# A hybrid decoder layer: four reciprocal square roots moved to GpSimd's power, and the sums of head norm and LayerNorm given out one at a time

## The chip, the cores and the metric

One core of one Trainium2 chip runs the whole program as one launch. The metric is the time of one execution on the device, in microseconds (us). The core's engines are called PE (TensorE, with its weight loads as PEld), DVE (VectorE), ACT (ScalarE), POOL (GpSimd) and SP (SyncE, which here issues the DMAs).

## The reference

One layer of a decoder is computed in fp32 for a prompt of 1024 tokens and for 8 sample sequences of 8 tokens (1088 tokens in all), with 1024 features:

```python
h = rmsnorm(x, norm_mix_pre)                      # x * rsqrt(mean(x*x) + EPS) * g
(a_b, a_c, a_u, b_p, c_q, c_f, c_i, c_g, d_a, d_g) = jnp.split(h @ w_in, 10, axis=-1)   # G = 256 each
ya = a_b * causal_dwconv(a_c * a_u, ...)          # A: short gated conv
yb = pooled @ w_grp * pool_scale                  # B: multi-scale pooling
# C: a scan with a matrix state, then per head (4 heads of 64):
o  = o * lax.rsqrt(jnp.mean(o * o, axis=-1, keepdims=True) + EPS) * norm_g
yc = o * jax.nn.silu(zg)
# D: GLU, 31-tap conv, then LayerNorm and swish
yd = jax.nn.silu(layernorm(conv + conf_b, conf_ln_g, conf_ln_b))
x  = x + rmsnorm(jnp.concatenate([ya, yb, yc, yd], axis=-1) @ w_out, norm_mix_post)
h  = rmsnorm(x, norm_ffn_pre)
x  = x + rmsnorm((jax.nn.silu(h @ w_gate) * (h @ w_up)) @ w_down, norm_ffn_post)
```

The outputs are x and the final states of the mixers.

## The kernel before

Features lie on the partitions in tiles of 128 and tokens lie along the free axis. Large products take three passes: an operand is split into a high part (`xh`, `wop`'s first half) and a low part (`xl`, `wop`'s second half), and the products high by high, high by low and low by high are summed in PSUM. The program runs through these stages:

- **Norm of x.** The 1088 tokens are cut into three chunks of 256, 384 and 448. `x_sq` squares a chunk on ACT (L217), `x_norm` makes the reciprocal square root of each token's mean square and scales the rows (L68), and `x_split` transposes them on PE (L234) and splits them into `xh` (ACT, L235) and `xl` (DVE, L71).
- **Phase 1, input projection and mixers.** Twenty units of 128 columns of `w_in` are multiplied (L984; a set of three products on 256, 384 and 448 tokens for each contraction tile and pass). The mixers' work on the other engines is written as Python generators. After every few products `hook` lets them run for about as long as the products take; a generator that must wait for another engine yields `None` and goes on at a later turn. PE and DVE keep the order in which this code issues their instructions (`tc.manual_schedule`); the orders of ACT and SP in this phase are set by a scheduler.
- **Mixer sums.** `stats_rstd` sums squares over features for each token: nine small products (L394) into a PSUM tile `sm`, of which there are two, and then `rsqrt_steps`. It serves the head norm (`hd`, once for each half j of the heads) and the LayerNorm (`ln`). `L916` is the last state update of mixer C; its result, also in an `sm` tile, is added to the state `s` on DVE.
- **Outputs of the mixers.** The last unit takes its contraction tiles in the order 6, 7, 2, 3, 0, 1, 4, 5, and `put_y` replaces `xh` and `xl` of a tile by the split outputs of the mixers (ACT cast L1030, DVE subtraction `xl<-y,xh` L65) once the unit is through with it. The last unit's own result is a gate (`z`, ACT L434) that is multiplied into an output tile by three DVE instructions `y<-y,z`.
- **Phase 2, output projection** (L1116): for the first token piece, one output tile after another takes the contraction tiles in the same order. The weights' halves are split by ACT (L1007) and DVE (`wop<-raw,wop`).
- **FFN.** Gate, up and down projections by Strassen's scheme and plain products (the groups at L1388 and L1593). The last token chunks of 448, 384 and 256 end in `finish`: token sums of squares on PE (L1082), a reciprocal square root (`rs_f0`, `rs_f1`, `rs_f2`), its transposition to all partitions on PE (`spread`, L178), scaling by the gain and the residual on DVE and POOL, and a store. In this last stage ACT, DVE, PE and POOL all keep the written order.

`rsqrt_steps` makes the reciprocal square root on DVE: one instruction for the argument m, two for an integer seed, and three Newton steps of three instructions, 12 in all, each working on the result of one just before it.

Of the kernel before, what the change touches and what calls it, by code (L numbers as in the profile page):

```python
# [13 lines left out]
ALU = mybir.AluOpType  # L14
# [3 lines left out]
P = 128  # L18
SEQ = 1024
NB, TB = 8, 8            # sample sequences, tokens of each  # L20
NT = SEQ + NB * TB       # 1088 tokens in all, the prompt's first
D = 1024
KT = D // P              # 8 feature tiles of the model
G = 256
NF = 22                  # hidden tiles of the FFN
EPS = 1e-6
F_MIN = 1e-20
CH = [(0, 256), (256, 384), (640, 448)]     # token chunks, one PSUM bank each
NG = SEQ // P            # 8 prompt groups of 128 tokens; the sample's 64 are group 8
GRP = [(i * P, P) for i in range(NG)] + [(SEQ, NB * TB)]  # L30
GO = [i * P for i in range(NG)] + [NT - P]     # groups of 128 tokens, the last overlapping
PW = 272
NPAIR = 8                                  # pairs of hidden tiles that go through the down projection by Strassen
HG = [range(16, 19), range(19, 22)]        # groups of the other hidden tiles
DC = [(0, 448), (448, 384), (832, 256)]     # token chunks of the down projection
PIECES = (0, 544, 272, 816)                # token pieces, as pairs of the two halves
# [3 lines left out]
# columns of the packed per-feature parameters  # L40
# [7 lines left out]
# columns of the constants that depend on shapes alone  # L48
# [4 lines left out]
def body(ctx, tc, xn, xT, win, wout, wgu, wdn, par, con, msk, poolw, s_conv, s_pool, s_hgrn, s_conf,  # L53
# [40 lines left out]
    V.memset(ones, 1.0)  # L94

# [4 lines left out]
    def rsqrt_steps(src, shape, scale, tag):  # L100
        """1 / sqrt(src * scale + EPS) on a compact tile: integer seed and three Newton steps."""
# [20 lines left out]

    def load_w(src, kt=4):
        raw = T(wp, [P, 4 * P], "raw").rearrange("p (k c) -> p k c", c=P)
        SY.dma_start(raw, src)
        return raw

    def split_w(raw, hl):
        """Weights into their high and low parts."""
        S.copy(hl[:, 0], raw)  # L130
        TT(hl[:, 1], raw, f32(hl[:, 0]), ALU.subtract)

    def mm_part(ps, hls, k, c):
        """One contraction tile's three passes on one token chunk."""
# [5 lines left out]
    # =====================================================================================  # L140
    # phase 1: input projection and the four mixers
    # =====================================================================================
# [20 lines left out]
    # lower bound of the forget gate: softmax over the one layer, its running sum less its first row  # L163
# [12 lines left out]
    def bcast(ps, col, n, off=0):  # L176
        """A per-token column to all partitions, feature-major."""
        PE.transpose(ps[:, off:off + n], col[:n].to_broadcast([n, P]), ident[:n, :n])  # L178
# [18 lines left out]
    # RMSNorm of x by tokens, then to feature-major and split; x lies where the mixers' outputs come later  # L197
# [22 lines left out]
    def x_norm(c, ss):  # L220
        idx = x_idx(c)
        for r in rsqrt_steps(ss[:, :len(idx)], [P, len(idx)], 1.0 / D, f"x{CH[c][1]}"):
            yield
# [76 lines left out]
    # A generator yields what its last step costs the vector engine, None where it has to wait for another engine.  # L300
    # The work of crit comes first, that of bulk fills what is left; due is what the last products call for.
    MM = 0.1135                               # a product's share of the schedule, one piece wide
# [3 lines left out]
    def fill(work, blocked):  # L306
        """A step of the first work that has any; what it costs."""
# [12 lines left out]
    def hook(budget):  # L320
        """As much of the other engines' work as fits under a stretch of products."""
# [23 lines left out]
    def until(ready):  # L345
        """Work without products until a condition holds."""
# [8 lines left out]
    def take(**want):  # L355
        """Waits for free buffers of the rings and counts them as taken."""
# [8 lines left out]
    def pe(cost):  # L365
        """The tensor engine's time for small products, in which the vector engine may do more."""
        state["budget"] += cost
# [21 lines left out]
    def stats_rstd(sq, scale, tag, rhs=None, w=1):  # L389
        """Sums over features of feature-major tiles, per token, then their rsqrt: [tokens, group * w]."""  # L390
        yield from take(sm=1)
        st = sm()
        for i, go in enumerate(GO):
# [3 lines left out]
            if i % SP == SP - 1:  # L397
                yield None
# [10 lines left out]
    # masks and state tiles  # L409
# [7 lines left out]
    qz = [T(mp, [P, 2, 256], f"qz{i}") for i in range(2)]      # each head's queries among zeros of the other's  # L417
# [6 lines left out]
    def pchunks(ps):  # L424
        """The prompt's part of a unit's products, chunk by chunk."""
# [180 lines left out]
    def b_pool(j, p, s):  # L606
        yield from wait(2 * LW)
        yield from take(h=2)
        # doubling sums; the last step only where the partition's window asks for it
# [80 lines left out]
    def hgrn(j):  # L690
# [12 lines left out]
        # blocks of four tokens, the decay taken relative to each block's second token  # L703
        for hf, (o, n) in enumerate(((0, 512), (512, NT - 512))):
# [21 lines left out]
            # their masked products; the heads' halves of the array work side by side  # L726
# [27 lines left out]
        # prefix products to q, suffix products to k, in blocks that double  # L754
# [1084 lines left out]
```

## Time and profile before

| quantity | value |
|---|---|
| median of 3 runs (lowest to highest) | 1198.31 us (1196.83 to 1198.78) |
| span of the profiled execution | 1193.7 us |
| median less that span | 4.6 us |
| PE busy | 1153.1 us, 97% |
| DVE busy | 885.4 us, 74% |
| ACT busy | 451.0 us, 38% |
| POOL busy | 139.9 us, 12%, 130 instructions |
| chain that ended last, by engine | PE 81%, DVE 10%, issue 3%, DMA 2%, ACT 2%, POOL 1% |

The span reaches from the profiled execution's first instruction to its last. No total beyond the span is given for that one execution, so steps are taken against the span, and the 4.6 us up to the median is taken as a constant. In the page's slices PEclk is the clock that was granted to PE, in tenths of full speed: it reads 9 in nearly all of the 40 slices and 8 in the 11th and in the last. A line such as `342.52 1.89 DVE L65 ... x3` gives the start and the length of a stretch of three instructions of one kind, both in us, and a bracket behind it gives the idle time before and what ended it. Where a matmul is busy, its start and end overlap its neighbours'.

### The profile page before, as it was taken

What the parts mean: (1) busy time and instruction counts of PE and PEld (TensorE: products, weight loads), DVE (VectorE), ACT (ScalarE), POOL (GpSimd) and SP (SyncE); (2) the same over time, 40 slices, a digit from 0 to 9 for tenths busy, and PEclk for the clock granted to TensorE, in tenths of its full rate; (3) what the DMA queues carried; (4) which work ended last, traced back from release to release, by engine and by line L of the source; (5) the groups of instructions that cost most, each with busy time, mean ns of one, the idle gap of its engine ahead of it and who ended that gap; (6) DMA issues with size and microseconds to landing.
All of it is one profiled execution on the core that took longest, in us unless ns stands there. A gap on an engine that the chain in (4) does not pass through costs nothing.

```text
span 1193.7 us, 21654 instructions
## 1 busy us (share of the span) xinstructions
PE 1153.1 (97%) x8476; PEld 1116.1 (94%) x8476; DVE 885.4 (74%) x1770; ACT 451.0 (38%) x964; POOL 139.9 (12%) x130
## 2 busy tenths in 40 slices
PE   5999999999999999999999999999999999999995
PEld 4899899998999999999999999999999989999994
DVE  6468979997674678786677576666675679998687
ACT  7534322243264453443333233233334653333321
POOL 1000000000000000000000000000002363447234
PEclk9999999999899999999999999999999999999998
DMA  7011112211135123021323233133234453434732
GB/s 261 34 38 24 36 37 68 41 36 40 30 130 199 39 74 127 24 95 67 115 101 105 70 111 118 60 114 110 91 122 135 141 178 121 137 109 125 259 108 88
DMA packets 93333, 116.89 MB, mean 98 GB/s; under 512 B 23664, under 2 KB 62192, under 8 KB 93232
## 3 DMA queue, kind: packets, MB, share of 16 engines
q1 hardware_dynamic: 93232, 115.52, 30.1%
q8 instruction: 66, 1.08, 0.4%
q14 instruction: 35, 0.29, 0.1%
HBM read 86.61 MB, written 28.88 MB: 97 GB/s over the span
## 4 chain that ended last, share of the span: by engine, by line
PE 81%; DVE 10%; issue 3%; DMA 2%; ACT 2%; POOL 1%; SPq 0%; DVEq 0%; ACTq 0%; POOLq 0%
PE p L1388 30%; PE mm L984 18%; PE p L1116 8%; PE p L1593 7%; PE p L1297 5%; PE p L1481 4%; DVE wop L65 3%; DVE raw L65 2%; PE mm L137 2%; PE sm L798 2%; DVE t L65 1%; DMA raw<-wgu 1%; ACT wop L1007 1%; DVE xl L65 1%; DMA raw<-hx 1%
## 5 line engine op out<-in xcount | busy, mean ns | idle before, releaser
L65 DVE TENSOR_TENSOR wop<-raw,wop 128x512 fp32r<-128x512 f32 (+2 forms) x296 | 210.2, 722 | 137.9 <-ACT wop L1007 127.5
L1007 ACT CAST wop<-raw 128x512 fp32r<-128x512 f32 (+1 forms) x240 | 143.4, 604 | 267.0 <-PE p L1388 151.7
L1388 PE MATMUL p<-xh,wop 128*128 128x272 f32 x1216 | 235.1, 288 | 0.0
L1388 PEld LDWEIGHTS p<-xh,wop 128*128 128x128 f32 x1216 | 193.5, 188 | 0.0
L1388 PE MATMUL p<-t,wop 128*128 128x272 f32 x912 | 179.6, 290 | 1.7 <-DVE u L65 1.6
L984 PE MATMUL mm<-xh,wop 128*128 128x256 f32 (+2 forms) x864 | 178.5, 335 | 0.0
L1388 PE MATMUL p<-xl,wop 128*128 128x272 f32 x608 | 175.6, 289 | 0.0
L1388 PEld LDWEIGHTS p<-t,wop 128*128 128x128 f32 x912 | 145.6, 188 | 2.4 <-DVE u L65 2.4
L984 PEld LDWEIGHTS mm<-xh,wop 128*128 128x128 f32 x864 | 139.5, 190 | 6.6 <-issue 1.1
L1388 PE MATMUL p<-x,wop 128*128 128x272 f32 x456 | 131.4, 288 | 0.0
L1388 PEld LDWEIGHTS p<-xl,wop 128*128 128x128 f32 x608 | 114.4, 188 | 0.0
L1116 PE MATMUL p<-xh,wop 128*128 128x272 f32 x512 | 99.2, 290 | 2.0 <-DVE wop L65 2.0
L984 PE MATMUL mm<-xl,wop 128*128 128x256 f32 (+2 forms) x432 | 99.0, 338 | 0.0
L65 POOL TENSOR_TENSOR x<-raw,x 128x544 fp32r<-128x544 f32 (+3 forms) x18 | 24.9, 1389 | 626.4 <-ACT x L1521 613.1
L65 DVE TENSOR_TENSOR raw<-raw,raw 128x512 f32<-128x512 f32 (+1 forms) x123 | 83.7, 690 | 4.5 <-DMA raw<-wgu 3.3
L1388 PEld LDWEIGHTS p<-x,wop 128*128 128x128 f32 x456 | 85.9, 188 | 0.0
L1593 PE MATMUL p<-xh,wop 128*128 128x272 f32 x456 | 82.1, 288 | 2.3 <-DVE acc L65 1.2
L71 DVE SCALAR_TENSOR_TENSOR y<-u,prm,y 128x1024 f32<-128x1024 f32 (+1 forms) x68 | 82.6, 1224 | 2.2 <-ACT y L570 0.7
L1116 PEld LDWEIGHTS p<-xh,wop 128*128 128x128 f32 x512 | 81.0, 188 | 2.2 <-DVE wop L65 2.2
L1593 PE MATMUL p<-xl,wop 128*128 128x272 f32 x456 | 81.5, 288 | 1.2 <-DVE x L65 0.9
L1297 PE MATMUL p<-xh,wop 128*128 128x272 f32 x384 | 74.1, 289 | 0.0
L1116 PE MATMUL p<-xl,wop 128*128 128x272 f32 x256 | 73.9, 289 | 0.0
(322 smaller groups left out, 2021.0 us busy)
## 6 DMA issues: line engine op xcount, KB each, us to landing
raw<-wgu SPq DMA_DIRECT2D x88, 256.0 KB, 2.7
raw<-hx SPq DMA_DIRECT2D x56, 272.0 KB, 2.7
raw<-win SPq DMA_DIRECT2D x40, 256.0 KB, 3.0
hx<-x SPq DMA_DIRECT2D x64, 136.0 KB, 1.8
raw<-wdn SPq DMA_DIRECT2D x32, 256.0 KB, 2.9
raw<-wdn SPq DMA_DIRECT2D x32, 192.0 KB, 2.9
x<-xT SPq DMA_DIRECT2D x8, 544.0 KB, 6.2
x<-x SPq DMA_DIRECT2D x8, 544.0 KB, 3.0
```

Source lines behind the costliest of these rows:

```text
L65: (eng or V).tensor_tensor(out, a, b, op)
L71: (eng or V).scalar_tensor_tensor(out=out, in0=a, scalar=s, in1=b, op0=op0, op1=op1)
L137: PE.matmul(ps[c][:, :n], hl[:, wi, kk], X[k][:, o:o + n], start=k == 0 and wi == 0 and X is XH, stop=k == KT - 1 and wi == 1)
L798: PE.matmul(ps[:rows, g * P:(g + 1) * P], kk[:, o:o + rows], qz[hf][:, :, g * 64:(g + 1) * 64], start=True, stop=True, skip_group_check=True)
L984: PE.matmul(ps[c][:, :w], hl[:, wi, kk], X[k][:, o:o + w], start=k == order[0] and wi == 0 and X is XH, stop=k == order[-1] and wi == 1)
L1007: S.copy(hl[:, 0], raw)
L1116: PE.matmul(ps[nt][:, :PW], WO[nt][k // 4][:, wi, kk:kk + P], X[k][:, o:o + PW], start=k == korder[0] and wi == 0 and X is XH, stop=k == k ...
L1297: PE.matmul(ps[r][:, :PW], w[:, wi, (k % 4) * P:(k % 4 + 1) * P], X[k][:, o:o + PW], start=k == 0 and wi == 0 and X is XH, stop=k == KT - ...
L1388: PE.matmul(ps[:, :PW], wop[:, wi, kk * P:(kk + 1) * P], x(kk, xi), start=first and kk == 0 and wi == 0 and xi == 0, stop=kk == 3 and wi == 1,
L1481: PE.matmul(ps[:, :n], wd[:, wi, kk * P:(kk + 1) * P], hops[k][xi][:, o:o + n], start=first and kk == 0 and wi == 0 and xi == 0, stop=not ...
L1593: PE.matmul(ps[:, :PW], ws[name][wi][q], x[:, xi, pr], start=first and q == 0 and wi == 0 and xi == 0, stop=q == 1 and wi == 1, skip_group ...
```

## The change

The diff is cut to the lines that act (it also takes comments out, which shifts line numbers by about 12):

```diff
     ones = T(const, [P, P], "ones")
     V.memset(ones, 1.0)
+    mhalf = T(const, [P, 1], "mhalf")
+    V.memset(mhalf, -0.5)
...
+    def rsqrt_pow(src, shape, scale, tag):
+        m, y = T(const, shape, f"rs_{tag}m"), T(const, shape, f"rs_{tag}y")
+        TS(m, src, scale, EPS)
+        GP.tensor_tensor(y, m, mhalf[:, :1].to_broadcast(shape), ALU.pow)
+        return y
...
     def x_norm(c, ss):
         idx = x_idx(c)
-        for r in rsqrt_steps(ss[:, :len(idx)], [P, len(idx)], 1.0 / D, f"x{CH[c][1]}"):
-            yield
+        args = ss[:, :len(idx)], [P, len(idx)], 1.0 / D, f"x{CH[c][1]}"
+        if c == 0:
+            r = rsqrt_pow(*args)
+        else:
+            for r in rsqrt_steps(*args):
+                yield
...
     def stats_rstd(sq, scale, tag, rhs=None, w=1):
...
             pe(0.22)
-            if i % SP == SP - 1:
-                yield None
+            yield None
...
     def finish(c, sqa, x1t):
         o, n = DC[c]
         st, gr = stats(sqa, n)
-        for r in rsqrt_steps(st, [P, len(gr)], 1.0 / D, f"f{c}"):
-            yield
+        r = rsqrt_pow(st, [P, len(gr)], 1.0 / D, f"f{c}")
+        yield
         rb = spread(r, gr)
...
-            for _ in range((11, 1, 1, 2, 2, 1, 2, 0)[j]):
+            for _ in range((1, 1, 1, 2, 2, 1, 2, 0)[j]):
```

For the first chunk of x and for the three last norms, DVE makes m, and POOL raises it to the power -0.5 in one instruction on a tile of 128 partitions by 2 to 4 columns. In the loop over output tiles, the first tile's 11 turns for the last norm become one, so that the other steps of `finish` stand at the same output tiles as before. In `stats_rstd`, the generator now gives up its turn after every one of its nine sums, and not after every third.

The first place is the end of the program, the norm of the last 256 tokens (`rs_f2`), on DVE. Before:

```order
L68 TENSOR_SCALAR rs_f2m_13387<-p_13384 128x2 [waits PE_49]
L68 TENSOR_SCALAR rs_f2y_13389<-rs_f2m_13387 128x2 [waits DVE_49]
L68 TENSOR_SCALAR rs_f2h_13388<-rs_f2m_13387 128x2
L65 TENSOR_TENSOR rs_f2a_13390<-rs_f2y_13389 128x2 [waits DVE_49]
L65 TENSOR_TENSOR rs_f2a_13390<-rs_f2a_13390,rs_f2h_13388 128x2 [waits DVE_49]
L71 SCALAR_TENSOR_TENSOR rs_f2y_13389<-rs_f2a_13390,rs_f2y_13389 128x2 [waits DVE_49]
```

Two more such Newton steps follow there. After, on POOL at the same place (`acc` and `t` are residual additions, of the chunk before ahead of the power and of this chunk behind it):

```order
L65 TENSOR_TENSOR acc_1308_10252<-acc_1308_10252,xl_1681_12851 128x384 [waits DMAHW1_49,DVE_49,Pool_49]
L65 TENSOR_TENSOR acc_1309_10253<-acc_1309_10253,xl_1681_12851 128x384 [waits DVE_49,Pool_49]
L129 TENSOR_TENSOR rs_f2y_13354<-rs_f2m_13353,mhalf_76 128x2 [waits DVE_49]
L65 TENSOR_TENSOR t_0_1302_10246<-t_0_1302_10246,xh_1710_13106 128x256 [waits DMAHW4_49,DVE_49]
L65 TENSOR_TENSOR t_0_1304_10248<-t_0_1304_10248,xl_1711_13108 128x256 [waits DMAHW5_49,DVE_49]
```

Eleven DVE instructions are gone, and one on POOL stands between DVE's `rs_f2m` and PE's `spread`.

The second place is on PE, at the last state update of mixer C in the second half of the heads (`L916`, after: `L928`). The names `sm` with a number are PSUM tiles, `cst` marks a head-norm sum and `ones` a LayerNorm sum. Before:

```order
L984 MATMUL mm_2697<-xh_9_81,wop_2619 128x448
L916 MATMUL sm_2831<-z_2809,khat_2755 64x512 [waits DVE_49,PE_49,Activation_49]
L916 MATMUL sm_2831<-z_2809,khat_2755 64x512 [waits DVE_49]
L394 MATMUL sm_2840<-cst_72,h_1566 128x2 [waits PE_49,Activation_49]
L394 MATMUL sm_2840<-cst_72,h_1566 128x2 x2
L984 MATMUL mm_2695<-xh_10_82,wop_2619 128x256
```

After:

```order
L996 MATMUL mm_2857<-xh_6_79,wop_2711 128x448
L928 MATMUL sm_2877<-z_2842,khat_2798 64x512 [waits DVE_49,Activation_49]
L928 MATMUL sm_2877<-z_2842,khat_2798 64x512 [waits DVE_49]
L407 MATMUL sm_2886<-cst_72,h_1556 128x2 [waits DVE_49,PE_49]
L407 MATMUL sm_2835<-ones_74,h_2618 128x1
L996 MATMUL mm_2855<-xl_14_87,wop_2711 128x256
```

LayerNorm's tile `sm_2835` is in use when the head norm's sums begin, the state update holds the other tile, and the first head-norm sum now waits for DVE.

The third place is on DVE, between the mixers and the output projection. Before (tiles 82, 83, 78, 79, 76, 77, 80 and 81 of `xh` are contraction tiles 6, 7, 2, 3, 0, 1, 4 and 5):

```order
L65 TENSOR_TENSOR xl_18_90<-y_26_104,xh_10_82 128x1088 [waits Activation_49]
L65 TENSOR_TENSOR xl_19_91<-y_27_105,xh_11_83 128x1088 [waits Activation_49]
L65 TENSOR_TENSOR xl_14_86<-y_22_100,xh_6_78 128x1088 [waits Activation_49]
L65 TENSOR_TENSOR xl_15_87<-y_23_101,xh_7_79 128x1088 [waits Activation_49]
L65 TENSOR_TENSOR xl_12_84<-y_20_98,xh_4_76 128x1088 [waits Activation_49]
L65 TENSOR_TENSOR xl_13_85<-y_21_99,xh_5_77 128x1088 [waits Activation_49]
L65 TENSOR_TENSOR wop_3151<-raw_3153,wop_3151 128x512 [waits DMAHW7_49]
L65 TENSOR_TENSOR y_25_103<-y_25_103,z_3147 128x256 [waits DVE_49,Activation_49]
```

There, the other two `y<-y,z`, three `wop` and then `xl` of tiles 4 and 5 follow. After (every tile's number is one higher):

```order
L65 TENSOR_TENSOR xl_15_88<-y_23_102,xh_7_80 128x1088
L65 TENSOR_TENSOR wop_3135<-raw_3137,wop_3135 128x512 [waits DMAHW5_49]
L65 TENSOR_TENSOR y_26_105<-y_26_105,z_3131 128x256 [waits DVE_49,Activation_49]
L65 TENSOR_TENSOR y_26_105<-y_26_105,z_3131 128x384 [waits DVE_49,Activation_49]
L65 TENSOR_TENSOR y_26_105<-y_26_105,z_3131 128x448 [waits DVE_49,Activation_49]
L65 TENSOR_TENSOR wop_3136<-raw_3138,wop_3136 128x512 [waits DMAHW6_49]
L65 TENSOR_TENSOR wop_3148<-raw_3150,wop_3148 128x512 [waits DMAHW3_49,PE_49]
L65 TENSOR_TENSOR wop_3149<-raw_3151,wop_3149 128x512 [waits DMAHW4_49,PE_49,Activation_49]
L65 TENSOR_TENSOR xl_16_89<-y_24_103,xh_8_81 128x1088
L65 TENSOR_TENSOR xl_13_86<-y_21_100,xh_5_78 128x1088
L65 TENSOR_TENSOR xl_14_87<-y_22_101,xh_6_79 128x1088
L65 TENSOR_TENSOR xl_17_90<-y_25_104,xh_9_82 128x1088 [waits Activation_49]
```

The `xl` of contraction tiles 3, 0 and 1 now stand behind `y<-y,z` and the `wop`, together with tile 4's; only tiles 6, 7 and 2 stand ahead.

## Prediction

> **What bounds the kernel now.** The page comes first: busy time by engine, then the chain of work that ended last.
>
> ```profile
> PE 1153.1 (97%) x8476; PEld 1116.1 (94%) x8476; DVE 885.4 (74%) x1770; ACT 451.0 (38%) x964; POOL 139.9 (12%) x130
> ...
> PE 81%; DVE 10%; issue 3%; DMA 2%; ACT 2%; POOL 1%; SPq 0%; DVEq 0%; ACTq 0%; POOLq 0%
> ```
>
> PE bounds nearly all of the span. Taking DVE work away is therefore worth something only where PE waits for it, and a change of order costs where it makes PE wait. PE can also lose time while it counts as busy: at a lower granted clock. So the second view is the busy time by 4 us stretches around the mixers' sums (columns: stretch, its length, busy PE, PEld, DVE, ACT, POOL, granted clock, DMA share, GB/s).
>
> ```profile
> 304.00:308.00 4.00, 4.00 (x33) 3.94 (x32) 2.35 (x5) 0.00 (x0) 0.00 (x0) 1.00 0.41 69
> 308.00:312.00 4.00, 4.00 (x19) 3.91 (x19) 1.77 (x7) 0.62 (x1) 0.00 (x0) 0.52 0.00 1
> 312.00:316.00 4.00, 4.00 (x16) 3.80 (x17) 3.52 (x22) 0.06 (x1) 0.00 (x0) 0.63 0.00 0
> 316.00:320.00 4.00, 4.00 (x22) 3.29 (x21) 0.76 (x2) 2.67 (x4) 0.00 (x0) 1.00 0.38 131
> ```
>
> The clock falls to half soon after 308 and is back before 316. The loss is 4.00 x (1 - 0.52) + 4.00 x (1 - 0.63) = 1.92 + 1.48 = 3.4 us. What ran just ahead is in the timeline of PE, third view.
>
> ```profile
> 302.08 1.08 PE L916 MATMUL sm<-z,khat 64*64 64x512 f32 x4
> 303.08 0.83 PE L394 MATMUL sm<-cst,h 128*128 128x2 f32 x6
> ...
> 304.85 0.66 PE L984 MATMUL mm<-xh,wop 128*128 128x256 f32 x3
> 305.35 0.72 PE L394 MATMUL sm<-cst,h 128*128 128x2 f32 x6
> 305.93 0.81 PE L394 MATMUL sm<-ones,h 128*128 128x1 f32 x6
> 306.60 0.74 PE L984 MATMUL mm<-xh,wop 128*128 128x256 f32 x3
> 307.18 0.72 PE L394 MATMUL sm<-cst,h 128*128 128x2 f32 x6
> 307.77 1.06 PE L394 MATMUL sm<-ones,h 128*128 128x1 f32 x6
> ```
>
> PE is never idle here, but from 304.85 to about 308.2 there are only two sets of wide products (starts 304.85 and 306.60, about 0.5 us each until the next group starts), some 1.1 us in 3.4, or a third. The rest are sums 1 or 2 columns wide. The clock falls right behind it. I read this as a grant that follows how many columns pass through PE, and not the busy share, which was full.
>
> **The change, part by part.**
>
> *Sums one at a time, the clock.* Nine turns in place of three spread the 18 instructions of each norm's sums between sets of wide products: one sum (about 0.12 us of PE, from the 0.7 us of three) behind each set or two. No stretch of 3.4 us then holds two thirds of sums, and the drop at 308 should go: -3.4 us. Bounds: 0, if it moves to a neighbouring stretch, and -3.4.
>
> *Sums one at a time, PE's wait for a PSUM tile.* There are two `sm` tiles. With LayerNorm's sums started earlier and ending later, its tile is held when mixer C's last state update takes the other. Head norm's first sum stands right behind that update on PE, and must now wait until DVE has read it.
>
> ```profile
> 303.23 1.40 DVE L65 TENSOR_TENSOR s<-s,sm 64x512 f32<-64x512 f32 x2 [0.17 <-PE sm L916]
> ```
>
> Before, PE started the sums at 303.08 while DVE read until 303.23 + 1.40 = 304.63. After, PE stands still for those two additions; everything behind the sum in PE's order waits too. From 303.08 to 304.63 it is 1.55; the addition's start can come a little sooner against PE. I take +1.4, bounds 0.7 (one addition, the other under PE's tail) and 1.6.
>
> *The transition to the output projection.* As a later end of the generators, the order on DVE changes: `xl` of contraction tiles 3, 0 and 1 stand behind `y<-y,z` and the `wop` splits. The rows of before, DVE first, then the group of the wide `xl`, then PE:
>
> ```profile
> 341.12 1.48 DVE L65 TENSOR_TENSOR y<-y,z 128x256 f32<-128x256 f32 x3
> 342.52 1.89 DVE L65 TENSOR_TENSOR wop<-raw,wop 128x512 fp32r<-128x512 f32 x3
> 344.32 2.69 DVE L65 TENSOR_TENSOR xl<-y,xh 128x1088 fp32r<-128x1088 f32 x5
> ```
>
> ```profile
> L65 DVE TENSOR_TENSOR xl<-y,xh 128x1088 fp32r<-128x1088 f32 x7 | 9.0, 1291 | 2.0 <-ACT xh L1030 1.9
> ```
>
> ```profile
> 340.89 0.28 PE L1116 MATMUL p<-xh,wop 128*128 128x272 f32 x1
> 341.01 0.29 PE L1116 MATMUL p<-xl,wop 128*128 128x272 f32 x1
> 343.26 0.52 PE L1116 MATMUL p<-xh,wop 128*128 128x272 f32 x2 [1.96 <-DVE wop L65]
> ...
> 345.66 0.39 PE L1116 MATMUL p<-xl,wop 128*128 128x272 f32 x1
> ```
>
> Before, PE waits 1.96 us for the `wop` split and then runs on; the product at 345.66 is the first to need `xl` of tile 4, which DVE makes from 344.32 to about 345.6. After, three more `xl` of 1.29 us stand between, so that tile 4 is ready 3 x 1.29 = 3.9 us later. PE has 3 products of about 0.125 us for each tile, so nothing covers it: the first output tile needs all of these tiles, and the second stands behind it on PE. `y<-y,z` cannot start much sooner, since its `z` waits for PE's last products of phase 1. I take +3.8; bounds 3.0 and 4.1 (the stretch of five at 344.32 has 2.69 us for two tiles' width, 1.35 for one). The space that DVE gains ahead of 341.12 is idle and buys nothing.
>
> *The transition, the clock.* From about 340.9 PE would have, until tile 4 is ready 8.8 us later, 18 products for the six tiles ahead, at 0.125 us 2.3 us in all: a quarter, the rest idle. That is thinner than the third before 308 that brought the drop, so I expect one here, of about the length of one such stretch (3.4 us) at half clock: 1.7 us if all of it would have been busy. Part of it lies under DVE's `xl`, so +1.5; bounds 0 and 3.4 (a drop as long as the one before). [...]
>
> *The first chunk's norm.* The start is a chain that DVE, ACT and the DMAs share.
>
> ```profile
> 8.37 0.17 DVE L68 TENSOR_SCALAR rs_x256m<-ss 128x2 f32<-128x2 f32 x1 [3.92 <-ACT h L217]
> ...
> 10.54 1.42 DVE L68 TENSOR_SCALAR y<-y,rs_x256y 128x1024 f32<-128x1024 f32 x2
> ```
>
> ```profile
> 12.04 0.18 ACT L217 ACTIVATION_READ_ACCUMULATOR h<-y 128x1 f32 x1
> 12.53 0.47 ACT L235 ACTIVATE xh<-sm,prm 128x256 fp32r<-128x256 f32 x1 [0.30 <-PE sm L234]
> ```
>
> DVE's 11 instructions take until 10.54. A power of length d ends that wait at about 8.37 + 0.17 + 0.1 + d + 0.1. But ACT squares the next chunk until 12.22, and its `xh` at 12.53 waits only 0.30 for PE. So at most 0.3 is won, and nothing is lost up to d of about 1.8. I take -0.3; bounds -0.3 and, for a late POOL, see the rivals. The new memset on DVE lies in its idle 3.92 us.
>
> *The power itself* is not in the trace. The nearest rows on POOL, by form:
>
> ```profile
> L68 POOL TENSOR_SCALAR y<-y,rs_x448y 128x1024 f32<-128x1024 f32 x1 | 1.6, 1620 | 9.2 <-ACT xh L235 9.2
> ...
> L65 POOL TENSOR_TENSOR t<-t,x 128x256 f32<-128x256 f32 x1 | 0.7, 722 | 0.8 <-DVE t L71 0.8
> ...
> L555 POOL MEMSET u<- 128x2 f32 x2 | 0.2, 99 | 144.1 <-DVE y L71 128.6 <-DVE h L71 15.5
> ```
>
> An instruction of two columns takes 0.1 us, one of two operands and 256 columns 0.72. A power is longer for each element, but has 2 to 4 columns; I take d = 0.5, bounds 0.1 and 1.6.
>
> *The last norm.* Here nothing lies beside it.
>
> ```profile
> 1182.17 0.16 DVE L68 TENSOR_SCALAR rs_f2m<-p 128x2 f32<-128x2 f32 x1 [0.71 <-PE p L1082]
> ...
> 1185.08 0.87 DVE L71 SCALAR_TENSOR_TENSOR t<-t,prm,p 128x256 f32<-128x256 f32 x2 [0.78 <-PE p L178]
> ```
>
> ```profile
> 1184.35 0.69 PE L178 MATMUL p<-cst,rs_f2y 128*128 128x128 f32 x2 [2.22 <-DVE rs_f2y L71]
> ```
>
> ```profile
> 1179.06 2.13 POOL L65 TENSOR_TENSOR acc<-acc,xl 128x384 f32<-128x384 f32 x2 [0.94 <-POOL t L65]
> 1185.64 0.72 POOL L65 TENSOR_TENSOR t<-t,xh 128x256 f32<-128x256 f32 x1 [4.46 <-DVE t L71]
> ```
>
> From m's start to PE it is 1184.35 - 1182.17 = 2.18 us. After: 0.16 for m, about 0.1 to POOL (its `t` at 1185.64 starts 0.1 behind the first of two DVE `t`, 1185.08 + 0.44), d, and 0.06 to PE, so 0.32 + d, or 0.8. The gain is 1.86 - d: -1.4 us, bounds -1.8 and -0.3. POOL is free, since its additions end at 1181.19. For the other two last norms PE has products or DVE has work beside them: nothing, bounds 0 and -0.2.
>
> *Sum:* -3.4 + 1.4 + 3.8 + 1.5 - 0.3 - 1.4 = +1.6 us. The profiled span of 1193.7 becomes 1195.3, and with the 4.6 us up to the median (1198.31) the time is 1199.9.
>
> **The rivals.**
>
> *The clock holds at the transition.* Speaking for it: the stretches are not the same in kind, sums there and idleness here, and where a stretch begins is chance. The sum is +0.1, 1198.4.
>
> *The transition costs nothing.* If `y<-y,z` and the `xl` behind it were done before PE asks for them, the new order would be hidden, and the sum is -3.4 + 1.4 - 0.3 - 1.4 = -3.7, 1194.6. For it speaks that DVE has some 3.9 us less to do ahead of 341; against it, that `z` comes from PE's last products of phase 1 and DVE's order is fixed.
>
> *POOL is late.* A power of 2.5 us turns the last norm's -1.4 into +0.6; the start, decided from d of 1.8, loses 0.7. The sum of +1.6 becomes +1.6 + 2.0 + 1.0 = +4.6, 1202.9. Against it: the columns are few, and the instruction of 1.6 us has 1024. [...]
>
> *The change does not remove the drop:* +5.0, 1203.3, if the waits of 1.5 us thin out the same stretch.
>
> **How the numbers follow.** The forecast (clock falls at the transition) has 0.40, the clock holding at the transition 0.25, no transition cost 0.19, a late POOL 0.11 (slow 0.08, once 0.03), the old drop staying 0.05. A measurement of this kernel tells about 0.2%, 2.4 us. The forecast's own range is 1198.4 to 1201.8; a quarter of it is beyond 1200.7. Faster: 0.19, and 0.06 from the case of the clock holding, where the price of 3.8 may be too high: 0.25. Slower: a quarter of the forecast, 0.10, the last two rivals, 0.16, and 0.05 from the clock holding, where it may be too low: 0.31. Same: 0.44. The range is 1194.6 to 1203.2.
>
> **What would show it.** In the changed profile the granted clock near 308 should stay at 1.00 and dip once near 340 to 350; PE's first head-norm sum of the second half should wait about 1.4 us for `s<-s,sm`; PE should wait for `xl` four times, about 3.8 us, beyond the wait for `wop`; between `rs_f2m` and PE's L187 there should be 0.8 us with the power's own length in it; the first `xh` should start near 12.2. The prediction is wrong if PE's waits for `xl` are under 2 us, if the power takes over 1.6 us, or if the clock still falls before 320.

## The result, and the profile after

The changed kernel took 1206.38 us (median of 5 runs, 1201.11 to 1207.38) and the kernel before 1197.85 us in its 5; the ratio is 1.0067, with a 95% interval of 1.005 to 1.0084. The change makes the kernel some 8 us slower. The forecast was slower by 1.6 us, within a range that ends at 1203.2: the sign of the likeliest case was right, the size was far off.

The profiled execution has a span of 1205.2 us against 1193.7. PE is busy 1158.1 us in place of 1153.1, idle 47.1 in place of 40.6.

```profile
PE 1158.1 (96%) x8476; PEld 1119.0 (93%) x8476; DVE 880.6 (73%) x1727; ACT 450.1 (37%) x964; POOL 142.5 (12%) x134
...
PE 75%; DVE 10%; issue 6%; DMA 4%; ACT 2%; POOL 2%; SPq 0%; POOLq 0%; DVEq 0%; ACTq 0%
```

The stretches of 4 us around the mixers' sums, with the columns of before (the granted clock is the third number from the right):

```profile
304.00:308.00 4.00, 4.00 (x25) 3.27 (x23) 1.87 (x5) 1.57 (x5) 0.00 (x0) 1.00 0.02 4
308.00:312.00 4.00, 3.29 (x19) 2.08 (x17) 2.32 (x4) 0.63 (x1) 0.00 (x0) 1.00 0.00 0
312.00:316.00 4.00, 3.08 (x16) 3.03 (x17) 2.03 (x4) 0.00 (x0) 0.00 (x0) 0.74 0.68 137
316.00:320.00 4.00, 4.00 (x16) 3.87 (x16) 0.00 (x0) 0.00 (x0) 0.00 (x0) 0.50 0.16 60
```

The drop has not gone. It begins 5.7 us later, and PE is idle for 1.6 us just ahead of it, in the stretches 308 and 312. The waits of PE from 280 to 356 us (what waited, for what; us in total, times, longest):

```profile
PE p L1128 <- DVE wop L65: 2.0, 1, 2.0
PE sm L407 <- DVE s L65: 1.6, 1, 1.6
PE p L1128 <- DVE xl L65: 1.6, 4, 1.1
PE sm L881 <- DVE sbd L71: 1.0, 2, 0.7
```

In the kernel before the same list holds the 2.0 for `wop` alone. The wait at the head norm's first sum (L407) and those for `xl` are the forecast ones; 1.0 us at mixer C's products (L881) was not forecast.

The four powers on POOL, and PE's wait for the last one:

```profile
L129 POOL TENSOR_TENSOR rs_x256y<-rs_x256m,mhalf x1: 710/710/710, 8.5 to 8.5; 128x2 f32<-128x2 f32 x1
L129 POOL TENSOR_TENSOR rs_f0y<-rs_f0m,mhalf x1: 1031/1031/1031, 1148.9 to 1148.9; 128x4 f32<-128x4 f32 x1
L129 POOL TENSOR_TENSOR rs_f1y<-rs_f1m,mhalf x1: 864/864/864, 1175.1 to 1175.1; 128x3 f32<-128x3 f32 x1
L129 POOL TENSOR_TENSOR rs_f2y<-rs_f2m,mhalf x1: 708/708/708, 1195.1 to 1195.1; 128x2 f32<-128x2 f32 x1
```

```profile
1195.87 0.69 PE L187 MATMUL p<-cst,rs_f2y 128*128 128x128 f32 x2 [1.04 <-POOL rs_f2y L129]
```

PE waits 1.04 us there, against 2.22 before: the last norm gained 1.2 us.

To see what belongs to the kernel and what to the single execution, both kernels were profiled three times more (unchanged programs; their expectations stand under the fifth experiment). The times are in us and read from the first product of each stage in the traces; "half clock" is the sum of PE's stretches at half clock between 25 and 1165 us.

| | before: 4 profiles | after: 4 profiles | mean difference |
|---|---|---|---|
| first product of the output projection | 340.9, 337.1, 338.2, 337.5 | 343.5, 340.3, 343.8, 342.2 | +4.0 |
| its first 64 products | 10.5, 11.8, 11.8, 10.6 | 15.5, 16.1, 15.7, 16.7 | +4.8 |
| down projection, pairs (L1593, after: L1605) | 176.7, 177.0, 177.1, 178.1 | 181.1, 180.7, 178.5, 179.3 | +2.7 |
| behind PE's last product of the group at L1481 (after: L1493), with the last norm | 16.0, 16.5, 16.4, 16.2 | 15.1, 15.4, 15.1, 15.4 | -1.0 |
| half clock | 6.8, 3.4, 3.4, 0 | 13.7, 10.2, 13.7, 13.7 | +9.4 |
| span | 1193.7, 1192.8, 1194.1, 1193.3 | 1205.2, 1201.7, 1202.8, 1202.5 | +9.6 |

The stages not listed differ by -0.9 us in all.

### The profile page after: what moved, and what is told of

Read it like the earlier page. It is cut to its first block, busy times and chain, and to the rows that moved or that the text cites. A ratio compares the mean times of both kernels' runs of the same rounds, so it can differ in the third digit from the quotient of the medians.

```text
span 1205.2 us, 21611 instructions
## 1 busy us (share of the span) xinstructions
PE 1158.1 (96%) x8476; PEld 1119.0 (93%) x8476; DVE 880.6 (73%) x1727; ACT 450.1 (37%) x964; POOL 142.5 (12%) x134
## 4 chain that ended last, share of the span: by engine, by line
PE 75%; DVE 10%; issue 6%; DMA 4%; ACT 2%; POOL 2%; SPq 0%; POOLq 0%; DVEq 0%; ACTq 0%
PE p L1400 28%; PE mm L996 15%; PE p L1128 8%; PE p L1605 7%; PE p L1309 6%; PE p L1493 4%; DVE wop L65 2%; PE mm L146 2%; DVE raw L65 2%; PE sm L810 1%; DMA raw<-hx 1%; DVE y L71 1%; DMA h<-xn 1%; POOL xh L65 1%; DVE t L65 1%
## 5 line engine op out<-in xcount | busy, mean ns | idle before, releaser
L996 PE MATMUL mm<-xh,wop 128*128 128x256 f32 (+2 forms) x864 | 179.5, 335 | 0.0
L996 PEld LDWEIGHTS mm<-xh,wop 128*128 128x128 f32 x864 | 139.3, 190 | 6.1 <-issue 1.4
L996 PE MATMUL mm<-xl,wop 128*128 128x256 f32 (+2 forms) x432 | 98.6, 337 | 0.0
L1605 PE MATMUL p<-xh,wop 128*128 128x272 f32 x456 | 82.5, 289 | 3.2 <-DVE t L65 1.4
L1605 PE MATMUL p<-xl,wop 128*128 128x272 f32 x456 | 81.6, 289 | 1.3 <-DVE x L65 1.1
```

What stands on the lines that cost most here:

```text
L996: PE.matmul(ps[c][:, :w], hl[:, wi, kk], X[k][:, o:o + w], start=k == order[0] and wi == 0 and X is XH, stop=k == order[-1] and wi == 1)
L1605: PE.matmul(ps[:, :PW], ws[name][wi][q], x[:, xi, pr], start=first and q == 0 and wi == 0 and xi == 0, stop=q == 1 and wi == 1, skip_group ...
```

## The experiments

**1. Sums alone, powers alone.** The first is the kernel before with this edit, the second is the kernel after with it undone:

```diff
-            if i % SP == SP - 1:
-                yield None
+            yield None
```

> The kernel before with only the sums of head norm and LayerNorm given out one at a time; all reciprocal square roots stay on DVE. Theory A (the loss comes from the order that the sums bring): PE waits about 1.6 us at the first head-norm sum of the second half, the clock still falls once between 305 and 325, PE's wait for xl at the output projection is there, the first 65 products of the output projection take 5 us longer than before; in all 8 us slower than before, 1206. Theory B (the power on POOL disturbs the rest): about as before, 1198 to 1200. The down projection (first to last plain product of line 1593 in the kernel before) took 176.8 us before and 181.3 after; theory C says that this part varies from execution to execution with the DMAs, and then it falls anywhere from 176 to 182 here, whatever the change.

> The kernel after with the sums given out three at a time again; the four powers stay. Theory A: the start is 0.65 us shorter and the last norm 1.1 us, the order at the mixers' end is that of before, one clock drop near 308; 1.8 us faster than before, 1196. Theory B: the loss stays, 1203 or more, with PE's extra waits in the down projection. Theory C: the down projection takes anywhere from 176 to 182 us.

Measured: the sums alone gave a ratio of 1.0091 (1.0064 to 1.0118), the powers alone 0.998 (0.9967 to 0.9993). The loss is the sums' and the powers are a small gain. The sums alone have the wait of 1.6 us, 16.0 us for the first 64 products and two drops of the clock:

```profile
PE p L1115 <- DVE wop L65: 2.0, 1, 2.0
PE p L1115 <- DVE xl L65: 2.0, 4, 1.1
PE sm L394 <- DVE s L65: 1.6, 1, 1.6
PE sm L868 <- DVE sbd L71: 1.0, 2, 0.7
```

The powers alone did not have the drop at 308, though their order there is that of before. This was not what theory A said, and it made the clock a question of its own (below).

**2. The wait for the PSUM tile, taken away.** One more turn ahead of the head norm's sums, which puts six wide products between the state update and the first sum:

```diff
+        yield from wait(1)
         r = yield from stats_rstd(sqo, 1.0 / 64, "hd", rhs=headones, w=2)
```

> The kernel after with one more turn ahead of the head norm's first sum, so that six wide products of about 1.0 us stand between mixer C's state update and that sum. Theory A: PE's wait there falls from 1.6 to 0.6 us, the stretch is no longer thin, and the clock stays at full speed from 300 to 330; the first product of the output projection starts 4.4 us earlier than in the kernel after. Rival (the clock falls by chance of its window, not by this wait): the clock falls all the same, and that product starts 1.0 us earlier.

Measured: ratio to before 1.0058 (1.0043 to 1.0073). The wait fell to 0.2 us, more than forecast, and the clock held:

```profile
304.00:308.00 4.00, 4.00 (x28) 3.60 (x28) 2.67 (x4) 1.60 (x5) 0.00 (x0) 1.00 0.02 5
308.00:312.00 4.00, 4.00 (x25) 3.55 (x24) 2.56 (x5) 1.84 (x3) 0.00 (x0) 1.00 0.01 4
312.00:316.00 4.00, 3.79 (x23) 2.35 (x22) 2.29 (x5) 0.00 (x0) 0.00 (x0) 1.00 0.06 10
316.00:320.00 4.00, 4.00 (x29) 3.90 (x29) 0.53 (x1) 0.05 (x1) 0.00 (x0) 1.00 0.77 186
```

The output projection began at 341.6, only 1.9 us earlier than in the first profile of after, where 4.4 was expected; a drop of 3.4 us at 221.8, which that profile does not have, accounts for up to 1.7 of the rest. The transition was no shorter (16.7 us), and the ratio's interval overlaps that of the kernel after, so no gain in time is shown.

**3. The order of `xl` at the transition, restored.** A smaller planned cost for the subtractions puts tiles 3, 0 and 1 ahead of `y<-y,z` again:

```diff
-                yield n * 0.0011
+                yield n * 0.0004
```

> The kernel after with a smaller planned cost for put_y's subtractions (0.0004 in place of 0.0011 per column), which puts xl of contraction tiles 3, 0 and 1 ahead of the products y by z on DVE again. Theory A: PE's waits for xl (1.6 us and what the slow clock hides) go, the clock does not fall near 348, and the first 65 products of the output projection take 10.5 us as before in place of 15.5: 5 us faster than after. Rival (the clock falls by the wait for wop alone): 3.3 us faster, the clock still falls near 348.

Measured: ratio 1.0083 (1.0067 to 1.0099), and 15.7 us for the first 64 products. The expectation failed. PE's waits for `xl` did go, but the one for `wop` took all of them over:

```profile
PE p L1128 <- DVE wop L65: 5.0, 1, 5.0
```

```profile
336.23 0.68 DVE L71 SCALAR_TENSOR_TENSOR y<-h,prm,sm 128x448 f32<-128x448 f32 x1 [0.69 <-PE sm L954]
337.48 7.30 DVE L65 TENSOR_TENSOR xl<-y,xh 128x1088 fp32r<-128x1088 f32 x6 [0.58 <-ACT xh L1042]
344.70 0.68 DVE L65 TENSOR_TENSOR wop<-raw,wop 128x512 fp32r<-128x512 f32 x1
345.31 1.42 DVE L65 TENSOR_TENSOR y<-y,z 128x256 f32<-128x256 f32 x3
```

DVE begins its first `xl` at 337.48, 4.5 us ahead of PE's first product of the output projection (341.97), and works without a pause from there. The first `xl` in the kernel before and in the kernel after, on DVE:

```profile
331.92 1.29 DVE L65 TENSOR_TENSOR xl<-y,xh 128x1088 fp32r<-128x1088 f32 x1 [1.16 <-ACT xh L1030]
```

```profile
339.02 3.70 DVE L65 TENSOR_TENSOR xl<-y,xh 128x1088 fp32r<-128x1088 f32 x3 [0.57 <-ACT xh L1042]
```

In the kernel before it begins at 331.92, 9.0 us ahead of PE's first product (340.89), and PE's products of phase 1 cover six `xl`. In the kernel after it begins 4.5 us ahead, and so it does in all four profiles. So it is not the order: DVE comes to `xl` 4.5 us late, with the same work still to do.

**4. LayerNorm's sums alone, head norm's sums alone.** The kernel after, with one of the two three at a time:

```diff
-            yield None
+            if tag == "ln" or i % SP == SP - 1:      # the other kernel: "hd"
+                yield None
```

> The kernel after with only LayerNorm's sums one at a time; head norm's are three at a time again. Theory A2 (the transition is late because LayerNorm's result, and with it the first tiles that put_y splits, comes late, so that all of DVE's subtractions fall into the last us of phase 1 in whatever order): PE's first head-norm sum of the second half waits for nothing, the first 65 products of the output projection take 15 us as in the kernel after; about 3.4 to 5 us slower than before. Theory A (the order on DVE alone, or the wait for the PSUM tile, made the loss): without that wait 12 us or less for these products, and no slower than before.

> The kernel after with only the head norm's sums one at a time; LayerNorm's are three at a time again, still begun ahead of the head norm's. Theory A2: LayerNorm ends earlier, so that the first 65 products take 10.5 to 12.5 us; the wait of 1.6 us at the first head-norm sum of the second half stays. Between before and after, 1198 to 1201 by the clock's drops. Theory A: a long wait at the transition here as well, 15 us.

Measured: 1.0026 (1.0015 to 1.0036) with LayerNorm's, 1.0029 (1.0015 to 1.0044) with the head norm's. The two losses come apart. With LayerNorm's alone, PE's waits are these, the first 64 products take 16.8 us, and there is no wait at the sums:

```profile
PE p L1129 <- DVE wop L65: 2.4, 1, 2.4
PE p L1129 <- DVE xl L65: 1.1, 4, 0.6
```

With the head norm's alone, PE waits at the sums and the first 64 products take 12.0 us:

```profile
PE p L1129 <- DVE wop L65: 2.2, 1, 2.2
PE sm L407 <- DVE s L65: 1.6, 1, 1.6
PE sm L882 <- DVE sbd L71: 1.0, 2, 0.7
PE p L1129 <- DVE xl L65: 0.9, 2, 0.6
```

The last Newton step of LayerNorm's reciprocal square root on DVE, before and after:

```profile
315.39 0.17 DVE L71 SCALAR_TENSOR_TENSOR rs_lny<-rs_lna,rs_lny 128x9 f32<-128x9 f32 x1
```

```profile
328.12 0.16 DVE L71 SCALAR_TENSOR_TENSOR rs_lny<-rs_lna,rs_lny 128x9 f32<-128x9 f32 x1
```

How far this step and DVE's first `xl` stand ahead of the output projection's first product, in us of each kernel's first profile:

| kernel | that step | first `xl` | first 64 products take |
|---|---|---|---|
| before | 25.5 | 9.0 | 10.5 |
| after | 15.4 | 4.5 | 15.5 |
| LayerNorm's sums alone | 13.0 | 3.4 | 16.8 |
| head norm's sums alone | 23.9 | 8.5 | 12.0 |

Theory A2 holds: nine turns in place of three make LayerNorm end later; the tiles that depend on it (contraction tiles 6 and 7) are the first that `put_y` takes, and all the others queue behind them. No run put tiles 6 and 7 at the end of that order, which would be the direct test. The head norm's sums have a small part in the transition too: 12.0 us against 10.5 and 10.6 in the two profiles of before in which the clock held there. Both kernels have the four powers, which gain 0.2%, so that each half of the sums costs about 0.5%, and together they make up the 0.9% of the sums alone.

**5. The same kernels again.** Nothing is edited.

> The kernel before once more, for its parts' spread from execution to execution. Theory C (the down projection's length varies with the DMAs whatever the kernel): its 176.7 us of the first profile come out anywhere up to 181. Rival (the change lengthens it): 176.7 within 0.5. The clock's drop near 308: by the theory that its window's phase decides, it may be there or not.

> The kernel after once more. Theory C: the down projection, 181.1 us in the first profile, comes out anywhere from 176 to 181. Rival: 181.1 within 0.5. The transition's wait is as in the first profile, the first 65 products at 15 to 17 us by the place of the clock's drop.

> The kernel before, a third profile. In eight of the ten profiles so far the down projection takes either about 177 us (before twice, and LayerNorm's sums alone) or 180 to 181 (after twice, and three kernels with the head norm's sums one at a time). Theory C (chance of the DMAs): a length of 180 turns up in a kernel before as well, in one of its three repeats or two. Rival C2 (the change makes it longer, by how its earlier stages shift the engines against each other): 176.5 to 178.7 each time.

> The kernel after, a third profile. Theory C: a down projection of 177 us turns up here as well. Rival C2: 180 to 181.5 each time. The clock's drop between 300 and 325 is there in some profiles and not in others, with an output projection that begins 3.4 us apart (343.5 with, 340.3 without).

> The kernel before, a fourth profile; expected as for the third: theory C 177 to 181 us for the down projection, rival C2 176.5 to 178.7. The output projection begins at 337 without and at 340.9 with the clock's drop ahead of it.

> The kernel after, a fourth profile; expected as for the third: theory C 177 to 181 us for the down projection, rival C2 180 to 181.5.

The measured stages are in the table above. The drop near 308 is in one of the four profiles of before. The same four stretches in the second profile of before:

```profile
304.00:308.00 4.00, 4.00 (x34) 3.95 (x33) 1.67 (x4) 0.00 (x0) 0.00 (x0) 1.00 0.41 70
308.00:312.00 4.00, 4.00 (x27) 3.86 (x26) 3.14 (x16) 0.62 (x1) 0.00 (x0) 1.00 0.00 0
312.00:316.00 4.00, 4.00 (x22) 3.28 (x21) 2.92 (x15) 2.73 (x4) 0.00 (x0) 1.00 0.07 19
316.00:320.00 4.00, 4.00 (x30) 3.81 (x29) 1.42 (x4) 1.72 (x3) 0.00 (x0) 1.00 0.32 112
```

In two others the clock falls at the transition instead, for 3.4 us, and in one nowhere.

These rows leave the question what decides. In all 18 profiles taken the clock changed on a grid of 3.413 us (the window of the expectations), and it fell behind every full-speed stretch of the grid in which PE took 0.40 or less of the columns that wide products would have brought (22 of them, counted in the last section). The grid's place differs from execution to execution (PE's first change to full speed came at 15.5 to 20.0 us), so a stretch of that length can be slid over a trace to see at how many starts it is so thin:

- In the three profiles of before without the drop near 308, only starts within a span of 1.5 us give 0.40 or less there, which is 0.44 of the grid's period.
- In the second profile of after, the one without the drop near 314, the span is 2.1 us, 0.63 of the period, and so it is in the second profile of the sums alone.
- In experiment 2's profile no start between 298 and 320 gives less than 0.45. Of the stretches counted in the last section none at 0.45 or more was followed by a drop, and none came there.

So the change did not take the thin place away but put a wider one in its stead. The counts agree: 3 of 7 profiles of kernels with the order of before have the drop between 305 and 320 (before, the powers alone, experiment 7), and 6 of 8 with the head norm's sums one at a time and the wait of 1.6 us (after, the sums alone, experiment 3, the head norm's sums alone).

The down projection's length fits neither theory wholly. The 180 of after did not hold (178.5, 179.3), and one profile of before reached 178.1; yet no profile of before is as long as the shortest of after.

**6. What lengthens the down projection, and what the powers cost.** The powers alone and the sums alone once more, and the power for head norm and LayerNorm too:

```diff
-        for r in rsqrt_steps(st[:, :9 * w], [P, 9 * w], scale, tag):
-            if held:
-                give(sm=1)
-                held = False
-            yield -0.2
+        r = rsqrt_pow(st[:, :9 * w], [P, 9 * w], scale, tag)
+        give(sm=1)
+        yield -0.2
```

> The four powers with the sums three at a time, once more and with more rounds. Theory A2: 0.1 to 0.3% faster than before, the last norm 1.1 us shorter, the order at the mixers' end that of before. The down projection: 177 to 178.7 us if the powers have no part in its lengthening, 180 or more if they have.

> The sums one at a time without any power, a second profile. The down projection: 180 or more if the sums' order has a part in its lengthening, 177 to 178.2 if that was chance.

> The four powers and, by the same power on POOL, the reciprocal square roots of head norm (18 columns) and LayerNorm (9 columns), sums three at a time. The four powers measured 0.71 us for 2 columns, 0.86 for 3 and 1.03 for 4, on a line of 0.39 + 0.16 per column. Theory L (the cost goes by columns): 1.8 us for 9 and 3.3 us for 18. Rival (a fixed cost): about 1 us for each. In time: no slower than the four powers alone, since PE waits for neither, 1194 to 1197.

Measured: the powers alone 0.9984 (0.9972 to 0.9996), with a down projection of 178.3 us (178.6 in the first profile); the sums alone 179.9 (180.5). In this second profile of the powers alone the clock does fall, at 309.7, so here too the drop comes in some executions and not in others. All six powers gave a ratio of 1.001 (0.9994 to 1.0025), which is no difference from before, with single runs from 1190.64 to 1200.12.

```profile
L129 POOL TENSOR_TENSOR rs_hdy<-rs_hdm,mhalf x2: 3210/3700/4191, 194.0 to 305.2; 128x18 f32<-128x18 f32 x2
L129 POOL TENSOR_TENSOR rs_lny<-rs_lnm,mhalf x1: 1788/1788/1788, 308.3 to 308.3; 128x9 f32<-128x9 f32 x1
```

The power's cost goes by columns: 1.79 us for 9 and 3.2 for 18 lie on the line of 0.39 + 0.16 per column from 2, 3 and 4 columns; one of 18 took 4.2. The expected gain of this kernel did not come; in its profile PE waits 1.6 us at the head norm's sums here as well. The profiled execution is the one of 1190.64, and the clock held in it from 25 to 1165 us.

**7. A version that beats both.** The powers alone, with the second half of the first tile's output weights split first, the half that contraction tiles 6 and 7 use:

```diff
-        for h in range(2):
+        for h in ((1, 0) if n == 0 else (0, 1)):
             yield 0.6
             split2k(raws[h], WO[n][h])
```

> The four powers, sums three at a time, and the first output tile's weights split with the second half first, which is the half that the first contraction tiles (6 and 7) use. PE's wait of 2.0 us for wop becomes two parts, and six products of 0.75 us run in between: 0.7 us faster than the four powers alone if DVE's part decides, with the clock's fall near 340 less often; the same if the second wait grows by what the first loses.

Measured: 1193.82 us against 1196.38, ratio 0.9981 (0.9967 to 0.9994). It beats both kernels; against the powers alone (0.9984) the difference is within the intervals. PE's wait of 2.0 became two, 1.0 and 0.7:

```profile
PE p L1129 <- DVE wop L65: 1.0, 1, 1.0
PE p L1129 <- DVE xl L65: 0.7, 1, 0.7
```

Most of what the first wait lost came back as a wait for tile 4's `xl`. The clock held at the transition in this profile, though; it fell at 308.3.

## Why the prediction was wrong

Stage by stage, the forecast and the mean difference of the four profiles are, in us: up to the output projection -2.3 (-3.4 + 1.4 - 0.3) and +4.0; its first 64 products +5.3 and +4.8; the down projection 0 and +2.7; the end -1.4 and -1.0; the rest 0 and -0.9. The sums are +1.6 and +9.6, and most of what lies between them is in the first row. Two of the three signs that the prediction named for being wrong came: the clock falls before 320 in three of the four profiles, and PE waits less than 2 us for `xl` in all of them.

- **The clock at 308 (-3.4): wrong, and the largest miss.** The step took a drop of one profiled execution for a property of the kernel. One of four profiles of before has it. What belongs to the kernel is the thin place; whether a stretch of the clock's grid falls on it is chance (experiment 5). By the 0.44 of the period found there, taking the place away altogether would have been worth 1.5 us on average, an estimate, and not 3.4. The rival that it stays had 0.05, and its condition, the waits of 1.5 us, is just what happened: in all four profiles of after a state update, a wait of 1.6 us and two small sums make a new thin place, and in three of them the clock falls behind it. Experiment 2 took the wait away and the drop there went with it; its profile has no start with less than 0.45 there. On average PE ran at half clock for 3.4 us in before and 12.8 in after; counted at half of that, as if PE had been busy throughout, the change costs 4.7 us by the clock, not saves 3.4.
- **The wait for the PSUM tile (+1.4): right, 1.6.** The reason is right only in part. The step has LayerNorm's sums begin earlier and end later. They begin at 305.9 us in before and at 305.4 in after; what moved is mixer C's last state update, from 302.1 to 310.2, so that it now stands behind LayerNorm's first sum. With the head norm's sums alone it stands at 311.2 and the wait is there, with LayerNorm's sums alone at 301.6 and there is none. So the head norm's sums bring the wait, by delaying mixer C, and LayerNorm's later end is not needed for it. The same shift brought another 1.0 us at mixer C's products (L881 waiting for `sbd`), which stood in no step. The output projection is preceded by 4.3 us at half clock on average in after and by 1.7 in before, which is 1.3 us of loss. With the 2.6 us of waits this makes 3.9 of the 4.0 us by which it began later; the gain at the start is not in it.
- **The transition (+3.8 and +1.5): right in size, wrong in its reason.** Its 64 products took 4.8 us longer, 5.3 forecast, with a drop of the clock in all four profiles of after. The step said that the order on DVE, `xl` behind `y<-y,z`, is the cause and that DVE idles ahead of it. Experiment 3 restored the order and the time stayed, as DVE only comes to `xl` at 337.5 (339.0 in after). LayerNorm's later end is the cause (experiment 4). The parts were off too: PE's waits for `xl` are 1.6, 0.7, 1.6 and 1.6 us in the four profiles, not 3.8, and the rest is PE at half clock for 6.8 or 10.2 us, where 3.4 was forecast. That the totals agree is luck: the forecast counted three subtractions of 1.29 us behind `y<-y,z`, and what happened is a DVE that begins the same work 4.5 us late.
- **The first chunk's norm (-0.3).** PE's first transposition came at 10.03 for 11.35 us, and the first `xh` at 12.06 for 12.53. That is 0.5 us, more than the 0.3 that the step held possible, but 0.14 of it is there already in the root's argument, at 8.23 for 8.37. The first product of phase 1's driven units (L984, L996) stands at 53.4 to 54.6 us in the four profiles of before and at 53.4 to 53.8 in those of after, 0.4 earlier on average, which is less than the spread of before.
- **The powers.** 0.71 us for two columns, 0.5 taken; the last norm gained 1.2 in PE's wait and not 1.4. The rival of a late POOL, slow or late once, is out: the first power (0.71) is as short as the last (0.71), and it began at 8.48 us, 0.08 behind the end of DVE's argument (8.23 and 0.17). The chance of 0.03 for a POOL that is late once was the author's guess; no run shows such a delay, and the first power ended at 9.19, ahead of the 10.54 at which DVE begins to scale the rows in before.
- **The down projection (0): missing.** It is 2.7 us longer on average, with identical instructions on PE, DVE and ACT there. In the first profile of after PE is idle for 8.9 us of it, and in before for 6.2. What can be seen is that the landing of the first pair's weights, loaded behind the stores `hd<-hst` in SP's queue, keeps DVE waiting 1.9 us in two of four profiles of before and 2.7 to 2.8 in the others, and 3.2 to 4.4 in after; behind a wait of 2.9 us in the powers alone PE shows none for it, behind 3.7 it waits 0.5 us, behind 4.3 (the sums alone) 1.1 and behind 4.4 1.2. That is not the whole of it, as the second profile of the sums alone has a wait of 2.8 and takes 179.9. The powers have no part: alone they gave 178.3 and 178.6, the sums alone 179.9 and 180.5. All 18 profiles together show that the sums' order has one. The nine of kernels with the head norm's sums one at a time take 178.4 to 181.1 us, 179.8 on average; the nine others, LayerNorm's sums alone among them, take 176.7 to 178.6, 177.6 on average. Within one kernel the length varies by up to 2.6 us, but chance would hardly part two groups of nine like this. By what the head norm's sums lengthen a stage that begins some 600 us later stays open; that DMAs meet others there is not shown.
- **The base.** 4.6 us were added to the first profile's span to reach the median. In later runs that list both, an execution's own time is 1.7 to 2.2 us above its span, so the profiled execution of before took an estimated 1195.6, less than any of the runs that were shown then.
- **Two readings.** The step on the sums took 0.12 us of PE for one sum; that is one instruction, and a sum is two of them, 0.24. And from PE's first product at 340.89 to tile 4's `xl` 3.9 us later than 345.6 it is 8.6 us, not 8.8. Neither changes the forecast.

Of the chances, "faster" and "same" had 0.69, mostly on the strength of the clock's -3.4.

## What to carry to other kernels

Before a drop of the clock is booked as a gain, see whether a second and a third profile of the same kernel have it, slide a stretch of the length found here (3.413 us) over the trace to see at how many starts it is thin, and look whether the edit leaves such a stretch somewhere else. A yield between small steps does not only spread work, it moves the end of everything that waits for the result: ask which later queue begins with that result, and how much work stands behind it. If two waits follow one another on a saturated engine, restoring an order may only change the name of the wait.

## What the runs showed of the hardware

- **The clock fell behind stretches with few columns, on a grid of 3.413 us.** In the first profile of before the clock stood at full speed for 290.13 and 866.99 us and between them at half for 6.83, which is 85, 254 and 2 times 3.413; in the first of after it stood at full speed for 296.96, 27.31 and 839.68 us and at half for 6.83 twice, which is 87, 8, 246 and 2 times. In 18 profiles, between 25 and 1165 us, the time was cut into stretches of 3.413 us on this grid, and the columns that passed through PE were counted against the wide products' rate (1088 columns in 0.495 us). All 22 full-speed stretches at or below 0.40 were followed by half clock, and of the 5928 others, at 0.41 and more, only one was (0.43). In the two first profiles the stretches ahead of half clock have 0.34 (at 304.8 us, before), 0.33 and 0.29 (at 310.5 and 344.6, after), and all others 0.43 or more. All stretches at half clock lasted 3.41, 6.83 or 10.24 us. In one execution of before the stretch at 304.8 has 0.34 and the clock falls; in another the stretch at 305.9 has 0.44 and it holds, with the same instructions. PE was busy all through the stretch at 304.8 (4.00 of 4.00 us from 304 and again from 308). The grid's place against the kernel's start varies: PE's first change to full speed lies at 18.04 us in the first profile of before, at 16.93 in that of after and anywhere from 15.5 to 20.0 in the 18, and all later changes are whole multiples of 3.413 us behind it.
- **A power on POOL costs 0.39 us and 0.16 for each column**, measured from 2 to 18 columns, except that one of the two with 18 columns took 4.2 us; there is no extra time at the first call (0.71 us at 8.5 us into the program).
